# Moving three quarters of the z projection between the convolved blocks, and one exponential with one fp32 value matmul per score tile in the banded attention

## The chip, the core and the metric

The kernel runs on one core of one Trainium2 chip. The metric is device time in microseconds (us) of one execution; smaller is better. The engines are TensorE (PE, with its weight loads shown apart as PEld), VectorE (DVE), ScalarE (ACT), GpSimd (POOL) and the queue that issues nearly all transfers (SP). Each engine takes its own instructions in the order in which the program has them.

## The reference, cut to what matters

Two layers of a hybrid trunk are computed for 1024 latent tokens and 128 context tokens (1152 together, nine tiles of 128). The change lies in the first layer, whose combined input projection yields queries, keys and values, a gate, z, the convolved channels xbc and dt:

```python
q, k, v, g, z, xbc, dt = split_cols(h @ w_in, (A_WIDTH, A_KV_WIDTH, A_KV_WIDTH, A_WIDTH, SSD_INNER, CONV_CH, 2 * SSD_HEADS))
xbc = silu(centred_conv(xbc, conv_w, conv_b))          # 1280 channels, 5 taps
# (A) attention in a band of 3 blocks of 128 keys, all 128 context keys and a sink logit, in one softmax
p = softmax([s_local, s_context, s_sink]);  attn = p @ [v_window, v_context]
# (B) two chunked state scans (forwards, backwards) over the convolved channels give y
a_out = attn * silu(g)
s_out = rms_norm(y * silu(z), gnorm_w)                 # z has 1024 columns
out   = concat([a_out, s_out]) @ w_out
```

The second layer (latent attention over all keys), the residuals and the final norm follow. All data are fp32.

## The kernel before

**Precision.** A product is made "whole" by splitting both sides into a high and a low part in the type fp32r (`split`, lines 249 to 253: ACT writes the high part, DVE the rest) and by three fp32r matmuls (`mm3`, lines 256 to 258). Some products are single matmuls in plain fp32 instead.

**Memory.** SBUF is divided by hand into four arenas, R, S, G and F; `Space.tile` takes a stretch of one, with `bufs` copies in turn. An instruction that rewrites a copy waits until the readers of the old one are done. `mem.set` opens an arena anew, after everything in the old one has ended.

**Order.** The program is written as generators that are woven together, and a scheduler then places the instructions of each engine, so rows of different generators stand mixed in one queue. Once placed, an engine's order is fixed.

**The stages around the change**, with the lines of the kernel before:

- Keys and values of all tiles, and the cached ones, are made first (`put_kv`); values are split into `VH` (with a column of ones, so that the value product also gives the softmax's denominator) and `VL`, in arena G.
- *Queries and z.* `weave(queries, 18, zproj, 36)` puts two z tiles beside each of 18 query tiles. A query tile (`query_tile`) is a projection of 24 matmuls of 256 columns, the rotation on DVE and POOL, a split, four transposes (L643), a copy by ACT (L644), eight score products `pp` (L660, L661), four maxima on DVE (L663), three small DVE steps (L667 to L669), and two small transposes (L672, L673) that write the negated maximum and the sink's exponential. A z tile (`zproj`) is 24 matmuls of 256 columns, a tanh (L686), one DVE step (L687) and a store; it is needed only in the scan.
- *Convolved blocks with attention.* `convs` runs over ten blocks of 128 channels. A block is three chunks of 24 matmuls of 384 columns (`fm_proj`), copied by ACT into the single buffer `ub` (L856 to L859), then a first tap on ACT (L878), four taps on DVE (L880), a tanh, transposes (L892), and chunk products of the states (`chunk_states`, L808, L812), whose results go to `H_d` (L840). Between blocks come pieces of `modulation` (L355, L356). Beside it runs `attention0`: per tile and key head two to four key blocks, each with a score tile of 128 by 512 (L740, L742, L743), two exponentials of the same score tile (L747 into fp32, L748 into fp32r), their difference `pl` (L749, on DVE or POOL in turn, one buffer), and three value matmuls into `acco` (L751 to L753). Three steps of attention go with one block. Its denominators go through memory (`den_d`, then `rd_d`).
- *Gates and first scans.* `gates0` makes 12 gate products. Each needs a chunk of matmuls (`fm_proj`, then the tanh of L713), the attention's output `ot` and a broadcast of `rd_d` into `rb` (L950; two buffers of `ot`, one of `rb`), a product on POOL (L951) and one on DVE (L953). `scan_out` for the context tile and the first latent tile is woven in, and `out_weights` loads the output weights.
- *Scans and output projection.* For each tile `scan_out` and `project_out`; the first transposes of `norm_T` (L1049) end the first tile of it.

The names in the rows are the arenas or the tiles: `acc` is a projection's PSUM tile, `sc` a score tile, `acco` the attention's sum, `pp` a score tile for the maxima, `st` the chunk states, `pt` a transpose.

Of the kernel before, what the change touches and what calls it, by code (L numbers as in the profile page):

```python
# [12 lines left out]
F32 = mybir.dt.float32  # L13
# [7 lines left out]
D = 1024  # L21
# [7 lines left out]
R_COLS, S_COLS, G_COLS, F_COLS = 27136, 4352, 11168, 9136  # L29
# [191 lines left out]
def hybrid_trunk(ctx: ExitStack, tc: tile.TileContext, I, O, dbg=None, stage=99):  # L221
# [243 lines left out]
    VH = kvp.tile([128, NB, 2, 65], F32R, name="VH", at="G")  # L465
    VL = kvp.tile([128, NB, 2, 64], F32R, name="VL", at="G")
    pool.memset(VH[:, :, :, 64:65].bitcast(F32), 1.0)

# [73 lines left out]
    with Space(mem) as p:  # L542
# [22 lines left out]
        def put_kv(p, blk, kr, vsrc):  # L565
# [12 lines left out]
            split(VH[:, blk, :, 0:64], VL[:, blk], vsrc.rearrange("p (h d) -> p h d", h=2))  # L578
# [102 lines left out]
        def zproj(zp, w):  # L681
            for q in range(4):
                for t in range(NT):
                    acc = tok_proj(t, w, 256)
                    th = zp.tile([128, 256], F32, tag="zth", name="zth", bufs=3)
                    act.activation(th, acc, AF.Tanh)  # L686
                    dve.scalar_tensor_tensor(th, th, 1.0, acc, ALU.add, ALU.mult)  # L687
                    dma.dma_start(z_d[t * 128:(t + 1) * 128, q * 256:(q + 1) * 256], th)
                    if t == 6 and q < 3:
                        wn = zw(q + 1)  # L690
                    yield
                w = wn

        with Space(mem) as qp:
            wp.widen("wh", "wl")
            weave(queries(qp, wq), 18, zproj(qp, wz), 36)

    if stage <= 2:
        dbg("KV", KH.bitcast(F32), KL.bitcast(F32), VH.bitcast(F32), VL.bitcast(F32), qm_d, es_d, dts)
        return  # L700
# [16 lines left out]
    def attention0(p):  # L717
# [4 lines left out]
        for t in range(NT):  # L722
            tok = slice(t * 128, (t + 1) * 128)
            for kv in range(2):
# [13 lines left out]
                for n, (kb, msk) in enumerate(blocks):  # L738
# [8 lines left out]
                    act.activation(pf, sc, AF.Exp, scale=SCALE_A)  # L747
                    act.activation(ph, sc, AF.Exp, scale=SCALE_A)  # L748
                    (pool if n % 2 else dve).tensor_tensor(pl, pf, ph.bitcast(F32), ALU.subtract)  # L749
                    vh = VH[:, kb, kv]  # L750
                    pe.matmul(acc[0:65], vh, ph, start=(n == 0), stop=False)  # L751
# [95 lines left out]
    def convs(p):  # L847
# [18 lines left out]
        for n, sb in enumerate(order):  # L866
            for b in range(2):
                w = ws.pop(0)
                ws.append(cw(2 * n + b + 2))
                for c in range(NCH):  # L870
                    evac(c, fm_proj(w, 0, hT, c))
                    for _ in range(4 + c):
                        next(beside, None)
# [816 lines left out]
```

## Time and profile before

| | |
|---|---|
| time of three runs | 1856.84, 1853.19, 1844.75 us; median 1853.19 us |
| profiled execution | 1854.25 us, its span 1852.5 us |
| PE busy | 1734.0 us (94%) in 9031 matmuls |
| DVE, ACT, POOL busy | 1043.6, 819.9, 744.5 us |
| mean granted TensorE clock | 0.956 |

The profile is one execution. A group row names the line, the engine, the operation, what it writes and reads, the count, then the busy time, the mean duration of one and the idle time ahead of it with what ended that. A row of the timeline gives the start in us from the span's start and the duration in us. Ends of matmuls are modelled and overlap with the next one, so what a matmul costs is read from the distance between starts. A plain fp32 matmul shows as two records, an fp32r matmul as one.

### The profile page before, as it was taken

To read this page: it belongs to the slowest core of one execution; us is meant where nothing else is said; L and a number is where in the kernel's file an instruction comes from. 1 tells how busy PE (TensorE), PEld (TensorE's weight loads), DVE (VectorE), ACT (ScalarE), POOL (GpSimd) and SP (SyncE) were. 2 spreads that over 40 slices of the span, in tenths; PEclk is the share of its full clock that TensorE was granted. 3 is DMA by queue.
4 is the path that set the end of the run, shared out by engine and by line. 5 is a ranking of instruction groups with operands and counts; after the bars stand their busy time and mean duration, and the time that the engine had idled before them with its cause. 6 is when DMAs were issued, how large, how long until landed. Compare 5 with 4: busy or idle time off the path is not lost.

```text
span 1852.5 us, 27066 instructions
## 1 busy us (share of the span) xinstructions
PE 1734.0 (94%) x9031; PEld 1314.2 (71%) x9031; DVE 1043.6 (56%) x1989; ACT 819.9 (44%) x1873; POOL 744.5 (40%) x741
## 2 busy tenths in 40 slices
PE   6899999999998888989899999999999999999898
PEld 3799999877775776767688898655565665554486
DVE  5665545655545467677665434655655556565243
ACT  5532323665655354444444422444544544545321
POOL 3510000133333345575633010456565575476432
PEclk9999999999998888998999998899999999999999
DMA  7423323444435697464463532020120121113352
GB/s 259 124 84 92 118 67 107 130 115 122 122 92 146 201 288 241 163 207 146 157 186 85 166 113 79 17 55 23 45 77 24 40 62 46 43 34 113 95 165 91
DMA packets 210655, 210.26 MB, mean 114 GB/s; under 512 B 36162, under 2 KB 175504, under 8 KB 210516
## 3 DMA queue, kind: packets, MB, share of 16 engines
q1 hardware_dynamic: 210372, 208.40, 37.6%
q8 instruction: 72, 1.18, 0.3%
q14 instruction: 67, 0.55, 0.1%
q0 software_dynamic: 144, 0.13, 0.0%
HBM read 151.94 MB, written 51.72 MB: 110 GB/s over the span
## 4 chain that ended last, share of the span: by engine, by line
PE 67%; DMA 11%; DVE 6%; ACT 3%; POOL 3%; issue 2%; SPq 2%; POOLq 0%; DVEq 0%; ACTq 0%
PE acc L256 12%; PE acc L258 12%; PE acc L257 12%; PE acco L1465 6%; PE pp L1427 3%; PE sc L1448 3%; PE sc L1450 3%; PE sc L1449 3%; DMA arenaG<-cum_d 2%; DMA arenaF<-rd_d 2%; DVE arenaR L250 2%; DMA arenaG<-rd_d 2%; PE st L808 1%; DMA rd_d<-arenaF 1%; PE yacc L1011 1%
## 5 line engine op out<-in xcount | busy, mean ns | idle before, releaser
L256 PE MATMUL acc<-arenaR 128*128 128x384 f32 (+4 forms) x1248 | 427.4, 343 | 19.4 <-ACT arenaR L249 9.1
L1478 POOL TENSOR_TENSOR arenaG<-arenaG 128x512 f32<-128x512 f32 x256 | 331.0, 1307 | 245.1 <-ACT arenaG L1455 178.8
L257 PE MATMUL acc<-arenaR 128*128 128x384 f32 (+3 forms) x1176 | 398.7, 339 | 0.1
L258 PE MATMUL acc<-arenaR 128*128 128x384 f32 (+4 forms) x1152 | 387.6, 338 | 0.2
L256 PEld LDWEIGHTS acc<-arenaR 128*128 128x128 f32 x1248 | 241.4, 194 | 60.8 <-ACT arenaR L249 11.6
L1455 ACT ACTIVATE arenaG<-sc 128x512 f32<-128x512 f32 (+1 forms) x304 | 175.5, 581 | 223.5 <-PE sc L1450 209.9
L209 DVE TENSOR_REDUCE arenaF<-pp 128x1 f32<-128x384 f32 (+1 forms) x400 | 198.5, 540 | 116.9 <-PE pp L1427 115.9
L257 PEld LDWEIGHTS acc<-arenaR 128*128 128x128 f32 x1176 | 226.8, 193 | 14.6 <-issue 2.7
L258 PEld LDWEIGHTS acc<-arenaR 128*128 128x128 f32 x1152 | 222.8, 193 | 16.6 <-DVE arenaR L250 2.2
L1465 PE MATMUL acco<-arenaG 128*64 128x512 f32 (+1 forms) x608 | 162.5, 614 | 1.1 <-ACT arenaG L1455 1.1
L250 DVE TENSOR_TENSOR arenaR<-arenaF,arenaR 128x512 fp32r<-128x512 f32 (+2 forms) x135 | 113.0, 851 | 60.5 <-ACT arenaR L249 55.9
L1005 ACT ACTIVATE arenaG<-arenaG,arenaF 128x128 f32<-128x128 f32 x288 | 88.7, 392 | 117.8 <-POOL arenaG L1003 117.5
L249 ACT CAST arenaR<-arenaF 128x512 fp32r<-128x512 f32 (+3 forms) x151 | 91.8, 626 | 92.3 <-DMA arenaF<-in_ab_w_in_dram 23.9
L749 POOL TENSOR_TENSOR arenaG<-arenaF,arenaG 128x512 fp32r<-128x512 f32 x28 | 48.4, 1728 | 149.8 <-PE acco L753 78.3
L1427 PE MATMUL pp<-arenaR 96*128 96x384 f32 (+1 forms) x300 | 96.1, 391 | 8.1 <-DVE arenaF L209 7.9
L1427 PEld LDWEIGHTS pp<-arenaR 96*128 96x128 f32 x300 | 57.9, 202 | 63.2 <-issue 27.3
L1448 PE MATMUL sc<-arenaR 96*128 96x512 f32 (+1 forms) x228 | 96.7, 424 | 3.6 <-ACT arenaG L1455 3.6
L258 PE MATMUL acc<-arenaR,arenaS 128*128 128x512 f32 (+1 forms) x240 | 92.2, 389 | 0.0
L1450 PE MATMUL sc<-arenaR 97*128 97x512 f32 (+1 forms) x228 | 89.9, 398 | 1.0 <-DMA arenaR<-arenaF 1.0
L1449 PE MATMUL sc<-arenaR 96*128 96x512 f32 (+1 forms) x228 | 89.4, 392 | 0.0
L1003 POOL TENSOR_SCALAR_AFFINE_SELECT arenaG<-arenaG 128x512 f32<-128x512 f32 x72 | 60.9, 869 | 65.7 <-DMA arenaG<-cum_d 53.4
L1448 PEld LDWEIGHTS sc<-arenaR 96*128 96x128 f32 x228 | 43.6, 191 | 59.5 <-ACT arenaG L1455 42.1
(328 smaller groups left out, 3362.7 us busy)
## 6 DMA issues: line engine op xcount, KB each, us to landing
arenaF<-in_ada_w_dram SPq DMA_DIRECT2D x96, 256.0 KB
arenaG<-cum_d SPq DMA_DIRECT2D x36, 512.0 KB
arenaF<-in_ab_w_in_dram SPq DMA_DIRECT2D x51, 256.0 KB
z_d<-arenaF SPq DMA_DIRECT2D x36, 128.0 KB
xs_d<-arenaF SPq DMA_DIRECT2D x8, 576.0 KB
arenaF<-xs_d SPq DMA_DIRECT2D x9, 512.0 KB
arenaF<-z_d SPq DMA_DIRECT2D x9, 512.0 KB
x_d<-arenaG SPq DMA_DIRECT2D x9, 512.0 KB
```

The lines of the kernel that those rows point to most:

```text
L209: f()
L250: lo_eng.tensor_tensor(lo, src, hi.bitcast(F32), ALU.subtract)
L256: pe.matmul(out, ah, bh, start=first, stop=False)
L257: pe.matmul(out, ah, bl, start=False, stop=False)
L258: pe.matmul(out, al, bh, start=False, stop=last)
L1427: pe.matmul(pp[:, 0:w], AQ[s][0:96, t * 128:(t + 1) * 128], AK[s][0:96, k0:k0 + w], start=True, stop=True)
L1448: pe.matmul(sc[:, 0:n], AK[s][0:96, ks], BQ[s][:, qs], start=True, stop=False)
L1449: pe.matmul(sc[:, 0:n], BK[s][:, ks], AQ[s][0:96, qs], start=False, stop=False)
L1450: pe.matmul(sc[:, 0:n], AK[s][:, ks], AQ[s][:, qs], start=False, stop=True)
L1455: act.activation(pf, sc[:, 0:n], AF.Exp, scale=SCALE_M)
L1465: (pinned if a == 0 else lambda f: f())(lambda: pe.matmul(acc[0][a * 64:(a + 1) * 64], V[:, a], pfs[a], start=(i == 0), stop=last))
L1478: pool.tensor_tensor(totals[a], first[a] if i == 1 else totals[a], pfs[a], ALU.add)
```

## The change

Five things are done together.

1. z: only the first quarter of its columns (256) stays beside the queries, so `weave` has 9 z tiles instead of 36. The other 768 columns are made in six blocks of 128 inside `convs`, one after each of the convolved blocks number 2 to 7 of ten: three chunks of 24 matmuls of 384 columns (`fm_proj`), tanh and DVE step on 128 by 384, three transposes per chunk, a copy by ACT into `zt`, and a store. The weights come as slabs of 128 columns in one list with those of the convolved blocks.
2. Attention: one exponential into fp32 (three buffers), no difference, and one plain fp32 value matmul per key block instead of three fp32r ones.
3. Values: one fp32 tile `VV` in arena F (copied by ACT) instead of `VH` and `VL` in G.
4. Two steps of attention instead of three go with one step of `convs`.
5. Arena G has 8576 instead of 11168 columns and F the 2592 more; three tiles and one reservation of the second layer may lie in G or F.

```diff
-R_COLS, S_COLS, G_COLS, F_COLS = 27136, 4352, 11168, 9136
+R_COLS, S_COLS, G_COLS, F_COLS = 27136, 4352, 8576, 11728
...
-    VH = kvp.tile([128, NB, 2, 65], F32R, name="VH", at="G")
-    VL = kvp.tile([128, NB, 2, 64], F32R, name="VL", at="G")
+    vvp = Space(mem, right=True)
+    VV = vvp.tile([128, NB, 2, 65], F32, name="VV")
...
-            split(VH[:, blk, :, 0:64], VL[:, blk], vsrc.rearrange("p (h d) -> p h d", h=2))
+            act.copy(VV[:, blk, :, 0:64], vsrc.rearrange("p (h d) -> p h d", h=2))
...
         def zproj(zp, w):
-            for q in range(4):
-                for t in range(NT):
-                    acc = tok_proj(t, w, 256)
...
+            for t in range(NT):
+                acc = tok_proj(t, w, 256)
...
-            weave(queries(qp, wq), 18, zproj(qp, wz), 36)
+            weave(queries(qp, wq), 18, zproj(qp, wz), 9)
...
-                    pf = p.tile([128, 512], F32, tag="pf", name="pf", bufs=2)
-                    ph = p.tile([128, 512], F32R, tag="ph", name="ph", bufs=2)
-                    pl = p.tile([128, 512], F32R, tag="pl", name="pl", bufs=1)
+                    pf = p.tile([128, 512], F32, tag="pf", name="pf", bufs=3)
                     act.activation(pf, sc, AF.Exp, scale=SCALE_A)
-                    act.activation(ph, sc, AF.Exp, scale=SCALE_A)
-                    (pool if n % 2 else dve).tensor_tensor(pl, pf, ph.bitcast(F32), ALU.subtract)
-                    vh = VH[:, kb, kv]
-                    pe.matmul(acc[0:65], vh, ph, start=(n == 0), stop=False)
-                    pe.matmul(acc[0:64], VL[:, kb, kv], ph, start=False, stop=False)
-                    pe.matmul(acc[0:65], vh, pl, start=False, stop=(n == len(blocks) - 1))
+                    pe.matmul(acc[0:65], VV[:, kb, kv], pf, start=(n == 0), stop=(n == len(blocks) - 1))
...
-        cw = lambda n: slab(w0, 2304 + blocks[n] * 128, 128, bufs=3) if n < 10 else gate_weights(n - 10)
-        ws = [cw(0), cw(1)]
+        todo = [slab_of for n in range(10) for slab_of in [(2304 + blocks[n] * 128, None)] + ([(1280 + (n + 1) * 128, 0.5)] if 0 < n < 7 else [])]
...
+        def z_block(b, w):
+
+            def turn(c, th):
+                pt = psum("tr", "pt")
+                for i in range(3):
+                    pe.transpose(pt[:, i * 128:(i + 1) * 128], th[:, i * 128:(i + 1) * 128], ident)
+                zt = p.tile([128, 3, 128], F32, tag="zt", name="zt", bufs=1)
+                act.copy(zt, pt[:, 0:CH].rearrange("p (t c) -> p t c", t=3))
+                dma.dma_start(z_d.rearrange("(t p) c -> p t c", p=128)[:, c * 3:c * 3 + 3, b * 128:(b + 1) * 128], zt)
+            for c in range(NCH):
+                acc = fm_proj(w, 0, hT, c)
+                if turns:
+                    turns.pop()()
+                th = p.tile([128, CH], F32, tag="zth", name="zth", bufs=2)
+                act.activation(th, acc, AF.Tanh)
+                dve.scalar_tensor_tensor(th, th, 1.0, acc, ALU.add, ALU.mult)
+                turns.append(partial(turn, c, th))
...
                 some_modulation(p, 2 if b and n < 2 else 1)
                 yield
+                if 0 < 2 * n + b < 7:
+                    w = ws.pop(0)
+                    next_weights()
+                    z_block(2 * n + b + 1, w)
+                    yield
...
-            done = [next(at, StopIteration) is StopIteration for _ in range(3)]
+            done = [next(at, StopIteration) is StopIteration for _ in range(2)]
...
-            tiles.append(p7.tile([128, NKT, 2, 64], F32, tag="vv", name="vv", bufs=3, at="G"))
+            tiles.append(p7.tile([128, NKT, 2, 64], F32, tag="vv", name="vv", bufs=3, at="GF"))
```

The scheduler places the instructions, so three places of its order are shown, before and after. In the rows a line number is that of the kernel the row is of; in the changed kernel the score matmuls are L736, L738 and L739, the value matmul L742, z's transposes L870, the taps L900, the attention output's load L976 and the broadcast of `rd_d` L978.

**The query stage's end.** Before, PE between two query tiles, with z's matmuls (here the 256-column rows) on both sides of the transposes of one query tile:

```order
L256 MATMUL acc<-arenaS,arenaR 128x256
L672 MATMUL pt<-ident,arenaS 4x128
L643 MATMUL pt<-ident,arenaG 128x128 x4
L673 MATMUL pt<-ident,arenaF 4x128
L257 MATMUL acc<-arenaS,arenaR 128x256
L258 MATMUL acc<-arenaS,arenaR 128x256
```

After, PE in the last five query tiles: the last score products of one tile, the transposes, and the score products of the next:

```order
L660 MATMUL pp<-arenaG,arenaR 128x384
L661 MATMUL pp<-arenaG,arenaR 128x128
L672 MATMUL pt<-ident,arenaS 4x128
L643 MATMUL pt<-ident,arenaG 128x128 x4
L673 MATMUL pt<-ident,arenaF 4x128
L660 MATMUL pp<-arenaG 128x256
L661 MATMUL pp<-arenaG 128x128
```

After, DVE at the same place: the last maxima of the query stage's last latent tile, its small steps, and the taps of the first convolved block (L900), with the context tile's maximum (L653) among them:

```order
L663 ISA arenaF<-pp,arenaF 128x384
L663 ISA arenaF 128x1
L667 SCALAR_TENSOR_TENSOR arenaF<-arenaF 128x4
L668 TENSOR_SCALAR arenaS<-arenaF 128x4
L669 SCALAR_TENSOR_TENSOR arenaF<-arenaS,arenaF 128x4
L900 SCALAR_TENSOR_TENSOR arenaF<-arenaF,vecs 128x1154 x2
L653 TENSOR_REDUCE arenaF<-pp 128x4
L900 SCALAR_TENSOR_TENSOR arenaF<-arenaF,vecs 128x1154
```

The projections have gone from between the last query tiles; five chunks of the first two convolved blocks stand ahead of them instead, and the sixth behind them.

**The attention among the convolved blocks.** Before, PE with the value matmuls of two key blocks, and scores:

```order
L753 MATMUL acco<-arenaG 65x512
L751 MATMUL acco<-arenaG 65x512
L752 MATMUL acco<-arenaG 64x512
L740 MATMUL sc<-arenaR,arenaG 128x512
L743 MATMUL sc<-arenaG 128x512
```

After, PE with the value matmuls of two key blocks, transposes of a z block between them, scores of two key blocks, and a chunk of a projection:

```order
L742 MATMUL acco<-arenaF 65x512
L870 MATMUL pt<-ident,arenaF 128x128 x3
L742 MATMUL acco<-arenaF 65x512
L736 MATMUL sc<-arenaR,arenaG 128x512
L738 MATMUL sc<-arenaG 128x512
L739 MATMUL sc<-arenaG 128x512
```

Three value rows have become one, and z's transposes stand among them.

**The first loads of the gates.** Before, SP from results of the last convolved blocks (`H_d`, `xs_d`) to the first load for a gate (L948); the first broadcast of `rd_d` (L950) follows 12 rows later:

```order
L840 DMA H_d<-arenaS 64x8x128 x2
L895 DMA xs_d<-arenaF 128x9x128
L759 DMA o_d<-arenaS 64x2x128 x2
L764 DMA arenaF<-den_d 64x16
L301 DMA arenaG<-in_ab_w_in_dram 128x4x128
L948 DMA arenaG<-o_d 128x384
```

After, SP from the last denominators to the first broadcasts (L978), with weight loads of the input projection (`in_ab_w_in`) and of the modulation (`in_ada_w`) still among them:

```order
L753 DMA arenaF<-den_d 64x16
L301 DMA arenaF<-in_ab_w_in_dram 128x4x128 x2
L976 DMA arenaG<-o_d 128x384 x2
L757 DMA rd_d<-arenaF 64x16
L301 DMA arenaF<-in_ada_w_dram 128x2x256
L978 DMA arenaG<-rd_d 64x3x128
```

The broadcasts of three gate products stand ahead of the last two stores of z blocks (L873) now, and of the last stores of `H_d`. PE has the attention's last value matmul (L742) in the first chunk of the last three convolved blocks, where the last one (L753) stood behind all of them before.

More of the change, by code (lines that the diff above doesn't have):

```diff
@@ L681, in zproj @@
         def zproj(zp, w):
-            for q in range(4):
-                for t in range(NT):
-                    acc = tok_proj(t, w, 256)
[L685 to L692, printed above, removed]
+            for t in range(NT):
+                acc = tok_proj(t, w, 256)
+                th = zp.tile([128, 256], F32, tag="zth", name="zth", bufs=3)
+                act.activation(th, acc, AF.Tanh)
+                dve.scalar_tensor_tensor(th, th, 1.0, acc, ALU.add, ALU.mult)
+                dma.dma_start(z_d[t * 128:(t + 1) * 128, 0:256], th)
+                yield
         with Space(mem) as qp:
             wp.widen("wh", "wl")
-            weave(queries(qp, wq), 18, zproj(qp, wz), 36)
+            weave(queries(qp, wq), 18, zproj(qp, wz), 9)
     if stage <= 2:
-        dbg("KV", KH.bitcast(F32), KL.bitcast(F32), VH.bitcast(F32), VL.bitcast(F32), qm_d, es_d, dts)
+        dbg("KV", KH.bitcast(F32), KL.bitcast(F32), VV, qm_d, es_d, dts)
         return
@@ L863, in convs, with next_weights @@
         blocks = [sb * 2 + b for sb in order for b in range(2)]
-        cw = lambda n: slab(w0, 2304 + blocks[n] * 128, 128, bufs=3) if n < 10 else gate_weights(n - 10)
-        ws = [cw(0), cw(1)]
+        todo = [slab_of for n in range(10) for slab_of in [(2304 + blocks[n] * 128, None)] + ([(1280 + (n + 1) * 128, 0.5)] if 0 < n < 7 else [])]
+        def next_weights():
+            if todo:
+                c0, scale = todo.pop(0)
+                ws.append(slab(w0, c0, 128, scale=scale, bufs=3))
+            elif len(gws) < 2:
+                gate_weights(len(gws))
+        ws = []
+        next_weights(), next_weights()
+        turns = []
+        def z_block(b, w):
[11 more added lines that the diff above has]
+                th = p.tile([128, CH], F32, tag="zth", name="zth", bufs=2)
+                act.activation(th, acc, AF.Tanh)
+                dve.scalar_tensor_tensor(th, th, 1.0, acc, ALU.add, ALU.mult)
+                turns.append(partial(turn, c, th))
+                for _ in range(2 + c):
+                    next(beside, None)
         for n, sb in enumerate(order):
@@ L868, in convs @@
                 w = ws.pop(0)
-                ws.append(cw(2 * n + b + 2))
+                next_weights()
                 for c in range(NCH):
                     evac(c, fm_proj(w, 0, hT, c))
+                    if turns:
+                        turns.pop()()
                     for _ in range(4 + c):
@@ L898, in convs @@
                 yield
+                if 0 < 2 * n + b < 7:
+                    w = ws.pop(0)
+                    next_weights()
+                    z_block(2 * n + b + 1, w)
+                    yield
         yield from beside
@@ L916, in hybrid_trunk @@
     kvp.close()
+    vvp.close()
     if stage <= 3:
@@ L940, in hybrid_trunk @@
     wp.widen("wh", "wl", place=1)
+    for k in ("wh", "wl"):
+        wp.rings[k][1] = 0
     def gates0(p):
@@ L1453, in pair_main @@
                     steps.tick()
-                    pf = p7.tile([128, 512], F32, tag="pf", name="pf", bufs=6, at="G")[:, 0:n]
+                    pf = p7.tile([128, 512], F32, tag="pf", name="pf", bufs=6, at="GF")[:, 0:n]
                     act.activation(pf, sc[:, 0:n], AF.Exp, scale=SCALE_M)
@@ L1476, in rest @@
                             if i == 1:
-                                totals[a] = p7.tile([128, 512], F32, tag="pt", name="pt1", bufs=4, at="G")[:, 0:n]
+                                totals[a] = p7.tile([128, 512], F32, tag="pt", name="pt1", bufs=4, at="GF")[:, 0:n]
                             pool.tensor_tensor(totals[a], first[a] if i == 1 else totals[a], pfs[a], ALU.add)
@@ L1613, in hybrid_trunk @@
                     p9.reserve("at8", 2 * D, 1, None, F32R)
[L1614 removed]
+                    p9.reserve("or8", D, 2, "FG")
                 for _ in pair_main(pair, op, CHUNKS[c:c + 1]):
```

3 lines of the change are left out of this document (1 added, 2 removed).

## Prediction

> **What bounds the kernel now.** I read the page's shares first, then the five stretches from the queries to the first scans, then single rows.
>
> ```profile
> PE 1734.0 (94%) x9031; PEld 1314.2 (71%) x9031; DVE 1043.6 (56%) x1989; ACT 819.9 (44%) x1873; POOL 744.5 (40%) x741
> 106.00:314.00 208.00, 207.74 (x1653) 205.54 (x1654) 111.29 (x339) 61.42 (x175) 13.93 (x20) 1.00 0.31 93
> 314.00:555.00 241.00, 231.66 (x1268) 184.78 (x1268) 134.35 (x200) 144.92 (x285) 72.85 (x71) 0.99 0.40 115
> 555.00:590.00 35.00, 30.10 (x156) 21.69 (x155) 21.46 (x44) 21.93 (x43) 14.48 (x14) 0.90 0.46 124
> 590.00:710.00 120.00, 99.96 (x476) 83.87 (x475) 69.79 (x114) 53.04 (x126) 48.01 (x52) 0.83 0.80 237
> 710.00:746.00 36.00, 31.23 (x138) 23.46 (x137) 23.97 (x33) 16.28 (x45) 19.57 (x20) 0.86 0.74 239
> ```
>
> Columns of the stretches: bounds, length, busy time and count of PE, PEld, DVE, ACT and POOL, granted PE clock, DMA share, GB/s. PE bounds the kernel, but not evenly. Beside the queries (106 to 314) it has no gap; in the convolved blocks (314 to 555) it lacks 9.3 us; from 590 on it idles a sixth of the time at a clock of .83, while the transfers are busiest. So a matmul added before 555 costs its whole time, and what the kernel can win lies behind 555. What paces that end:
>
> ```profile
> L859 ACT COPY arenaF<-acc x10: 250/272/299, 301.9 to 554.6; 128x128 f32<-128x128 f32 x10
> L951 POOL TENSOR_TENSOR arenaG<-arenaG x12: 993/1056/1447, 610.4 to 707.9; 128x384 f32<-128x384 f32 x12
>   DMA arenaG<-rd_d: 34.6, 9
> L953 DVE TENSOR_TENSOR arenaG<-arenaG x12: 545/558/957, 611.5 to 708.9; 128x384 f32<-128x384 f32 x12
> L950 SPq DMA_DIRECT2D arenaG<-rd_d x24: 574/593/1561, 604.0 to 702.0; - x24
> L840 SPq DMA_DIRECT2D H_d<-arenaS x16: 580/596/637, 407.2 to 661.6; - x16
> L1049 PE MATMUL pt<-ident,arenaG x72: 270/273/421, 742.9 to 972.7; 128*128 128x128 f32 x72
> ```
>
> The numbers after the count are shortest, mean and longest in ns, then first and last start. The last convolved chunk leaves PE at 554.6. Of the gate products, 9 of 12 wait 34.6 us on POOL for the broadcast of rd_d, which has one buffer; they come (708.9 − 611.5)/11 = 8.85 us apart. Two chains end at L1049, 742.9: the gates, 34.0 us after the last L953, and the states, whose last store starts 107.0 us after the last chunk and leaves 81.3 us more.
>
> **What PE gets to do.** Costs come from starts, as ends overlap:
>
> ```profile
> 149.92 0.28 PE L256 MATMUL acc<-arenaS,arenaR 128*128 128x256 f32 x1
> 150.04 0.28 PE L257 MATMUL acc<-arenaS,arenaR 128*128 128x256 f32 x1
> 396.49 0.34 PE L258 MATMUL acc<-arenaR 128*128 128x384 f32 x1
> ...
> 397.90 0.33 PE L257 MATMUL acc<-arenaR 128*128 128x384 f32 x1
> 399.77 0.39 PE L753 MATMUL acco<-arenaG 128*65 128x512 f32 x1
> 400.00 0.40 PE L751 MATMUL acco<-arenaG 128*65 128x512 f32 x1
> 400.23 0.40 PE L752 MATMUL acco<-arenaG 128*64 128x512 f32 x1
> 400.47 0.34 PE L256 MATMUL acc<-arenaR 128*128 128x384 f32 x1
> 406.91 1.04 PE L892 MATMUL pt<-ident,arenaS 128*128 128x128 f32 x8
> 407.70 0.47 PE L753 MATMUL acco<-arenaG 128*65 128x512 f32 x1
> 739.47 2.08 PE L992 MATMUL off<-arenaG,arenaF 64*128 64x512 f32 x4
> 741.48 0.79 PE L256 MATMUL acc<-arenaR,arenaS 128*128 128x512 f32 x1
> 1501.80 1.08 PE L1465 MATMUL acco<-arenaG 128*64 128x512 f32 x4
> 1502.81 0.44 PE L1427 MATMUL pp<-arenaR 96*128 96x384 f32 x1
> ```
>
> *z.* A 256-column matmul takes .12 us. Of 384 columns, eight lie from 396.49 to 397.90, .176 each. Gone are 27 z tiles × 24 × .12 = 77.8 us; new are 18 chunks × 24 × .176 = 76.0 and 54 transposes, by L892's eight from 406.91 to 407.70 at .10, 5.3. Net +3.5.
>
> *Values.* Three fp32r matmuls (399.77 to 400.47) take .70 us. One plain fp32 matmul of 512 columns is two records: L992's four records, two matmuls, took 2.01 us together, 1.0 each. The narrow L1465 gives a lower end: its four records, two matmuls, took 1.01 together, but the two fill 64 columns each of the array side by side; each alone costs between .51 (its share) and 1.01 (if a neighbour is free). I take L992, the nearer in shape (full 512 columns, no neighbour): .31 more on each of 62 blocks, +19.2. The bounds are −12 (.51) and +21 (2.08/2, L992's busy time).
>
> The Trainium skill, page "FP8 and Floating Point Precision", section "TensorE Precision Notes", says that true FP32 takes four passes through the array. By that rule, four of the .23 us passes make .92, an estimate, +14 us instead of +19; this trace's 1.0 is a little above it. Either way three passes become about four.
>
> **The query stage loses its filler.** z stays beside only the first query tiles; five of the last have no projection between them.
>
> ```profile
> 150.16 0.34 PE L660 MATMUL pp<-arenaG 128*128 128x384 f32 x1
> 151.20 0.22 PE L661 MATMUL pp<-arenaG 128*128 128x128 f32 x1
> 153.57 0.17 DVE L668 TENSOR_SCALAR arenaS<-arenaF 128x4 fp32r<-128x4 f32 x1
> 156.22 0.27 PE L672 MATMUL pt<-ident,arenaS 128*4 128x128 f32 x1
> 156.33 0.60 PE L643 MATMUL pt<-ident,arenaG 128*128 128x128 f32 x4
> 156.97 0.59 ACT L644 CAST arenaR<-pt 128x512 fp32r<-128x512 f32 x1 [2.79 <-PE pt L643]
> L663 DVE CUSTOM_DVE_ANT_0 arenaF<-pp,arenaF 128x512 f32<-128x512 f32 (+1 forms) x64 | 38.8, 654 | 11.5 <-PE pp L661 11.0
> L880 DVE SCALAR_TENSOR_TENSOR arenaF<-arenaF,vecs 128x1154 f32<-128x1154 f32 x36 | 54.1, 1503 | 6.2 <-ACT arenaF L878 4.8 <-DMA arenaG<-qs_d 1.2
> ```
>
> One tile's loop is: first score product to the small step L668, 153.57 + .17 − 150.16 = 3.58; transposes, 156.97 − 156.22 = .75; the copy, .59: 4.9, with semaphores 5.0. PE has 1.8 of work in it (products 1.26, transposes some .5), and nothing else stands there in its order: 3.2 us idle, three times, 9.6 (I take the first two of the five as covered by what the queue still holds). The last tile is worse, since on DVE three taps of the first convolved block stand behind its last maxima, and the sixth chunk's buffer comes free only after them: four maxima at .65 and small steps, 3.6 in all, then four taps at 1.50, 6.0, and 1.2 for the buffer's copy and first tap, less 2.5 us of PE's own work there, is 8.3. Together +18. It is 0 if the five chunks ahead run late enough to cover them, and 24 at most (five tiles at 3.2 + the last).
>
> **The convolved stage gets its waits back.**
>
> ```profile
> L753 PE MATMUL acco<-arenaG x62: 387/397/690, 326.2 to 586.9; 128*65 128x512 f32 x62
>   POOL arenaG L749: 16.9, 10
>   DVE arenaG L749: 3.1, 9
> L747 ACT ACTIVATE arenaF<-sc 128x512 f32<-128x512 f32 x62 | 37.2, 600 | 31.8 <-POOL arenaG L749 17.8 <-DVE arenaG L749 9.7 <-PE sc L743 4.0
> 555.00:590.00 35.00, 3.96 (x9) 1.36 (x9) 0.90 0.46 124
> ```
>
> The third value matmul waits 20.0 us for the difference pl, mostly for POOL. That goes, and with it 62 of the exponentials of .6 and all differences. What is late next is the one exponential after the scores, behind z's 18 tanhs, copies and DVE steps on the same engines; ACT was busy 145 of 241 us here and ends lower. I take back 16 of the 20, since an exponential that ACT does late still stops PE; bounds 8 and 20.
>
> One thing more moves: 9 of 62 L753 ran behind the last chunk (the last row is the stretch 555 to 590 for L753 alone). With three score matmuls of the same width, 9 × (.70 + .69) = 12.5 us of PE work now come before it.
>
> So the last chunk leaves PE at 554.6 + 3.5 + 19.2 + 12.5 + 18 − 16 = **591.8**, 37.2 us later.
>
> **The end stage gains more than that.** Because the attention ends ahead of the last three blocks, three gate products have their loads issued before the last z stores and need only their chunk. *Gates:* of twelve, nine are left at 8.85 from the last chunk on, with 6 us to the first (the loads alone, without the 17 us of den_d and rd_d round trip): 6 + 79.7 = 85.7, at 677.5; then 34.0 as before, and 10 for work that PE did while it waited for broadcasts and now has left over (half of the 20 us that it idled from 590 to 710): 721.5. *States:* their last store came 107.0 after the chunk, with nine attention steps and all gates' weight loads between; the steps are gone, PE's idle there (20 of 120 us at .83) is partly closed, and I put it at 60, then 74 of the 81.3 as cum_d's loads start earlier: 591.8 + 134 = 725.8. That 60 is the softest number here, between 35 (only the states' own work, the stretch to 590) and 107 (nothing gained). The later of the two decides: 725.8 against 742.9, **−17.1**.
>
> *At nothing:* the values' split, now one ACT copy per tile, lies beside projections that PE works through without a gap (106 to 314); if that cover failed it would be a copy of .6 on nine tiles, 5. The smaller arena G costs the scans and the second layer nothing as long as no tile waits for an older reader longer than now; no row shows that, and I bound it by ±10. What follows L1049 has the same instructions and moves as a whole.
>
> 1854.25 − 17.1 = 1837.1 on the profiled execution; that one lies 1.1 above the median of three, so **1836**.
>
> **Rivals.** About 1% (18.5 us) is what a measurement of this kernel tells from no change; the forecast sits on that line.
>
> *More gain (chance .18).* The scheduler's five chunks really cover the query tiles, the 18 us go, and all behind comes 18 sooner: 1818. For: PE has no gap at all beside queries now. Against: the order's rows, where score products of one tile follow the transposes of the last with nothing between.
>
> *No gain (.16).* The transfers bind the end. From 590 to 746 the queues moved 120 us × 237 + 36 × 239 GB/s = 37 MB, at the highest DMA share of the five stretches; the change takes none of it away. At 237 GB/s from 591.8 it takes 156 us, to 747.8, 4.9 later than now: 1858. For: the broadcasts waited for are transfers. Against: in 314 to 590 the share is under .5, so what is issued earlier has room.
>
> *Slower (.16).* The first broadcast of rd_d still comes after the last chunk. Then the twelve are served as before: 17 us (604.0 − 586.9) of round trip, 12 × 8.85 = 106 and 44, from 596 (591.8 and the attention's last steps): 763, +20: 1873. It decides from the moment the first gate product on POOL starts later than the last chunk. Against it stand SP's rows; for it, that SP's rows only say what is issued in order, and a weight load ahead that waits for its buffer holds all behind.
>
> **Numbers.** Forecast .50, own range 1806 to 1850: below, values at .51 (−31 against my 1.01) bring 1805, say 1806; above, the tail at 24 and waits at 8 bring 1836 + 6 + 8. Half of it lies over the 1% bound of 1834.7. The range goes from 1806 to 1868, the no-gain rival and the arenas' 10: it holds the first two rivals and leaves out the slower one and a few ends, under .2. Faster .25 + .18 = .43; same .25 + .16 = .41; slower .16.
>
> **What would show it.** Value matmuls 1.0 apart in two records; PE gaps of 3 us between L661 and L672 in the last queries, 8 ahead of a chunk; waits of the value matmul under 4 us in all; the last L859's successor at 585 to 600; three gate products on POOL before it; L1049 near 726. Wrong if the first gate product lies behind the last chunk, if the chunk comes past 605, or if the arenas' new split (G is 2592 columns narrower) makes scans or the second layer wait for buffers, of which this trace shows nothing.

## The result, and the profile after

The changed kernel took **1912.33 us** (median of 4 runs, 1909.35 to 1915.84): 1.031 times the kernel before, 95% interval 1.027 to 1.035. I had forecast 1836, a gain of 1%; it lost 3%, outside my range. Times here and below are medians that leave out two slow executions, one each of the kernels with two buffers for `rd_d` and with a single broadcast. The profiled execution took 1909.35 us, its span 1907.2.

The stages, from the view of time stretches (bounds, length, busy time and count of PE, PEld, DVE, ACT, POOL, granted PE clock, DMA share, GB/s). First after:

```profile
PE 1758.0 (92%) x8807; PEld 1323.3 (69%) x8807; DVE 1009.4 (53%) x1936; ACT 798.3 (42%) x1820; POOL 692.6 (36%) x713
106.00:280.00 174.00, 148.86 (x1004) 139.55 (x1005) 94.04 (x300) 44.72 (x136) 13.83 (x20) 0.88 0.25 74
280.00:622.70 342.70, 336.47 (x1781) 273.94 (x1779) 135.31 (x223) 162.49 (x320) 44.65 (x55) 0.98 0.42 120
622.70:783.40 160.70, 132.66 (x662) 109.28 (x661) 102.47 (x159) 70.01 (x165) 67.84 (x71) 0.86 0.75 215
783.40:1025.10 241.70, 216.35 (x996) 168.51 (x995) 155.35 (x198) 97.95 (x271) 120.29 (x130) 0.90 0.52 164
```

Then before, the stretches that were not shown yet, cut at the same events: last convolved chunk, first and last transposes of `norm_T`.

```profile
314.00:554.60 240.60, 231.26 (x1266) 184.55 (x1266) 133.95 (x198) 144.69 (x285) 72.83 (x70) 0.99 0.41 116
554.60:742.90 188.30, 158.59 (x752) 126.58 (x750) 113.50 (x188) 89.24 (x207) 81.07 (x84) 0.85 0.73 218
742.90:972.70 229.80, 211.32 (x997) 165.63 (x996) 158.47 (x198) 100.14 (x279) 128.07 (x131) 0.93 0.55 171
```

Idle PE is length less busy time. What the clock costs I take as half of the time that PE is busy in the spans of half clock that the trace lists. The rest is work at full clock:

| stage (us) | before | after | difference | of it PE work | idle PE | half clock |
|---|---|---|---|---|---|---|
| 106 to the last chunk | 448.6 | 516.7 | +68.1 | +28.2 | +21.8 | +18.2 |
| to `norm_T`'s first transposes | 188.3 | 160.7 | −27.6 | −17.2 | −1.7 | −8.7 |
| scans, to its last | 229.8 | 241.7 | +11.9 | +2.1 | +6.9 | +2.9 |
| the rest | 879.8 | 882.1 | +2.3 | | | |

The milestones, by line: the last chunk's copy (L848), the gate products (L979), the states' stores (L829), `norm_T` (L1077).

```profile
L848 ACT COPY arenaF<-acc x10: 268/272/285, 236.3 to 622.7; 128x128 f32<-128x128 f32 x10
L979 POOL TENSOR_TENSOR arenaG<-arenaG x12: 992/1014/1443, 582.9 to 746.0; 128x384 f32<-128x384 f32 x12
  DMA arenaG<-rd_d: 15.3, 5
L829 SPq DMA_DIRECT2D H_d<-arenaS x16: 574/601/1477, 388.1 to 687.0; - x16
L1077 PE MATMUL pt<-ident,arenaG x72: 270/273/475, 783.4 to 1025.1; 128*128 128x128 f32 x72
```

**Where the query stage lost it.** The timeline of PE in the last query tiles (start, duration; in brackets the idle time before it and what ended it):

```profile
251.06 0.27 PE L672 MATMUL pt<-ident,arenaS 128*4 128x128 f32 x1 [2.33 <-DVE arenaS L668]
...
254.72 0.31 PE L661 MATMUL pp<-arenaG 128*128 128x128 f32 x1
256.55 0.37 PE L672 MATMUL pt<-ident,arenaS 128*4 128x128 f32 x1 [1.52 <-DVE arenaS L668]
256.71 1.06 PE L643 MATMUL pt<-ident,arenaG 128*128 128x128 f32 x4
257.57 0.42 PE L673 MATMUL pt<-ident,arenaF 128*4 128x128 f32 x1
258.45 0.69 PE L660 MATMUL pp<-arenaG,arenaR 128*128 128x384 f32 x1 [0.46 <-ACT arenaR L644]
...
274.32 0.37 PE L672 MATMUL pt<-ident,arenaS 128*4 128x128 f32 x1 [2.07 <-DVE arenaS L668]
...
275.30 0.52 PE L257 MATMUL acc<-arenaR 128*128 128x384 f32 x1
275.62 0.52 PE L258 MATMUL acc<-arenaR 128*128 128x384 f32 x1
...
279.49 0.34 PE L257 MATMUL acc<-arenaR 128*128 128x384 f32 x1
279.67 0.34 PE L258 MATMUL acc<-arenaR 128*128 128x384 f32 x1
140.00:220.00 80.00, 66.80 (x483) 63.26 (x481) 42.85 (x148) 18.05 (x58) 7.45 (x11) 0.91 0.24 71
251.40:278.70 27.30, 18.56 (x66) 14.56 (x65) 15.86 (x43) 6.98 (x21) 0.00 (x0) 0.50 0.26 76
```

The waits are those that I forecast, on DVE's small step L668 and ACT's copy L644. What I had left out is their second price: for 27.3 us (the last row) the clock is .50, and a matmul of 384 columns starts every .32 us (275.30 to 275.62) where it later takes .18. The wait of 3.2 us that I worked out per tile is 2.0 of idle PE here (1.52 + .46): of the 5.8 us from one L672 to the next (256.55 to 262.36) PE's own work takes 3.8, twice the 1.8 that I had. Nor is it the last tiles only: from 140 to 220 (the last row but one), while some z tiles still stood beside the queries, PE lacks 13.2 of 80 us at a clock of .91, with four spans of half clock of 3.4 us each.

### The profile page after: what moved, and what is told of

Same layout as the page of the kernel before. It is cut to its first block, busy times and chain, and to the rows that moved or that the text cites. A ratio compares the mean times of both kernels' runs of the same rounds, so it can differ in the third digit from the quotient of the medians.

```text
span 1907.2 us, 26407 instructions
## 1 busy us (share of the span) xinstructions
PE 1758.0 (92%) x8807; PEld 1323.3 (69%) x8807; DVE 1009.4 (53%) x1936; ACT 798.3 (42%) x1820; POOL 692.6 (36%) x713
## 3 DMA queue, kind: packets, MB, share of 16 engines
HBM read 151.94 MB, written 51.72 MB: 107 GB/s over the span
## 4 chain that ended last, share of the span: by engine, by line
PE 33%; DMA 8%; DVE 3%; ACT 3%; SPq 2%; issue 2%; POOL 0%; DVEq 0%; POOLq 0%; ACTq 0%
PE acco L1493 5%; PE acc L256 5%; PE acc L257 5%; PE acc L258 5%; PE pp L1455 3%; PE sc L1476 3%; PE sc L1478 3%; PE sc L1477 2%; DMA arenaF<-rd_d 2%; DMA arenaF<-in_mla_w_in_dram 1%; DMA rd_d<-arenaF 1%; ACT arenaR L249 1%; DMA arenaF<-in_mla_w_out_dram 1%; PE den L1522 1%; DVE arenaF L1300 1%
## 5 line engine op out<-in xcount | busy, mean ns | idle before, releaser
L256 PE MATMUL acc<-arenaR 128*128 128x384 f32 (+4 forms) x1248 | 440.8, 354 | 36.0 <-ACT arenaR L249 11.0
L257 PE MATMUL acc<-arenaR 128*128 128x384 f32 (+3 forms) x1176 | 409.6, 348 | 0.1
L258 PE MATMUL acc<-arenaR 128*128 128x384 f32 (+4 forms) x1152 | 399.4, 347 | 0.1
L1506 POOL TENSOR_TENSOR arenaG<-arenaG 128x512 f32<-128x512 f32 x192 | 248.6, 1306 | 233.0 <-ACT arenaG L1483 166.1
L256 PEld LDWEIGHTS acc<-arenaR 128*128 128x128 f32 x1248 | 243.6, 195 | 79.7 <-issue 22.9
L250 DVE TENSOR_TENSOR arenaR<-arenaF,arenaR 128x512 fp32r<-128x512 f32 (+2 forms) x140 | 121.3, 882 | 126.1 <-ACT arenaR L249 125.2
L785 POOL TENSOR_TENSOR arenaS<-arenaF 128x256 f32<-128x256 f32 x72 | 57.8, 826 | 326.3 <-ACT arenaF L913 165.4
L249 ACT CAST arenaR<-arenaF 128x512 fp32r<-128x512 f32 (+3 forms) x156 | 98.0, 646 | 149.5 <-DMA arenaF<-in_ada_w_dram 29.0
L1455 PEld LDWEIGHTS pp<-arenaR 96*128 96x128 f32 x300 | 57.8, 202 | 63.2 <-DVE arenaF L209 25.6
L250 DVE TENSOR_TENSOR arenaR<-acc,arenaR 64x384 fp32r<-64x384 f32 (+2 forms) x84 | 48.1, 578 | 58.2 <-ACT arenaR L249 57.3
L1033 ACT ACTIVATE arenaF<-arenaF 128x128 f32<-128x128 f32 x144 | 44.7, 389 | 77.7 <-POOL arenaF L1031 77.7
```

The costliest lines, as they stand in the source:

```text
L250: lo_eng.tensor_tensor(lo, src, hi.bitcast(F32), ALU.subtract)
L256: pe.matmul(out, ah, bh, start=first, stop=False)
L257: pe.matmul(out, ah, bl, start=False, stop=False)
L258: pe.matmul(out, al, bh, start=False, stop=last)
L1455: pe.matmul(pp[:, 0:w], AQ[s][0:96, t * 128:(t + 1) * 128], AK[s][0:96, k0:k0 + w], start=True, stop=True)
L1506: pool.tensor_tensor(totals[a], first[a] if i == 1 else totals[a], pfs[a], ALU.add)
```

## Experiments

Ratios are to the kernel before, with 95% intervals. "Stage" numbers are from each run's profile, cut at the same three events.

**z back beside the queries.**

```diff
-            weave(queries(qp, wq), 18, zproj(qp, wz), 9)
+            weave(queries(qp, wq), 18, zproj(qp, wz), 36)   # zproj of before
-                if 0 < 2 * n + b < 7:
+                if False:
-            done = [... for _ in range(2)]
+            done = [... for _ in range(3)]
```

> The changed kernel with z wholly beside the queries again (36 tiles) and three attention steps a block; the attention and the arenas stay changed. Theory 'filler' (the query stage of the changed kernel lost 25.1 us to idle PE and 15.4 us to the halved clock, 40.5 together): the last convolved chunk leaves PE 44 us or more earlier than its 622.7, at 565 to 580, and the kernel takes 1860 to 1878 us. Rival 'attention' (the plain fp32 value matmuls and the narrower arena make the loss): the kernel stays at 1895 us or above.

1857.21 us, **1.0036** (1.0014 to 1.0058). The stretch before the last chunk fell from 516.7 to 464.4 us; 'filler' holds, and the total is 3 us below its range.

```profile
106.00:316.00 210.00, 209.57 (x1666) 207.28 (x1666) 111.93 (x340) 62.53 (x181) 13.87 (x20) 1.00 0.31 93
570.40:733.10 162.70, 139.46 (x697) 113.70 (x696) 100.92 (x163) 74.30 (x173) 68.84 (x73) 0.87 0.74 218
```

PE has no gap in the first row, as before the change. The second says something that I had not asked: the end stage is as short (162.7) as in the changed kernel (160.7). So it does not need z between the blocks, and the next run shows that it does not need the new attention either. The attention's part of the change costs .36% with z beside the queries, and z's move the rest: 1.0309 / 1.0036 = 1.027.

**The z move alone.** The kernel before with the changed kernel's `zproj`, `z_block` and list of slabs, and two attention steps to a block; `zth` and `o` with one buffer.

> The kernel before with the z move alone: attention with two exponentials, a difference and three value matmuls, arenas of before, two attention steps to one of the blocks (to make room, z's tanh tile and the attention's sum copy have one buffer). Theory 'filler': the query stage loses about 40 us as in the changed kernel, and the total is 1880 to 1900 us. Rival 'attention': within 10 us of the kernel before, 1845 to 1865. A side question, the 12 us lost in the last scan tile: if they come from the narrower arena G, they are absent here and present in the kernel with z back.

1888.95 us, **1.0223** (1.0180 to 1.0266). As 'filler' had it:

```profile
106.00:281.00 175.00, 149.36 (x1019) 140.07 (x1018) 95.81 (x303) 45.30 (x138) 13.79 (x20) 0.89 0.25 73
618.10:766.00 147.90, 130.09 (x677) 106.19 (x675) 102.58 (x158) 69.97 (x165) 69.25 (x71) 0.93 0.78 233
766.00:1006.60 240.60, 216.32 (x994) 166.24 (x995) 156.11 (x199) 98.21 (x271) 120.75 (x130) 0.90 0.53 164
```

25.6 us idle and 14.1 lost to the clock in the first row. The side question is answered too: the scans (last row) took 240.6 us with the wide arena G of before, and 229.7 with the narrow one in the run with more work below, so the narrower arena is not what lengthened them. What the 236.6 with z back come from is not shown.

The end stage (second row) is 147.9 us with the old attention, shorter than in the changed kernel. What the short ones share is when the attention ends. Its last value matmul starts ahead of the last chunk's copy in all three: at 523.8 against 570.4 with z back, 558.4 against 618.1 here, 562.3 against 622.7 in the changed kernel. In the kernel before, 9 of 62 run behind it. That is the step that I forecast, but no run changes it alone.

**Half of z beside the queries.**

```diff
-            weave(queries(qp, wq), 18, zproj(qp, wz), 9)
+            weave(queries(qp, wq), 18, zproj(qp, wz), 18)   # two quarters
-                if 0 < 2 * n + b < 7:
+                if 0 < 2 * n + b < 5:
```

> The changed kernel with half of z (18 tiles) beside the 18 query tiles and half in four blocks among the convolved ones. Theory 'filler': each query tile finds one z tile, the query stage's 40.5 us of idle and halved clock fall to some 20, and the kernel takes 1885 to 1895 us. Rival 'tail' (only the last tiles without any z lose, 18 us as I had it): the nine z tiles more fill the last tiles too, the loss goes nearly whole, and the time is near that of the kernel with z wholly back.

1875.24 us, **1.0145** (1.0095 to 1.0195), 10 us less than 'filler' had and 18 more than with z wholly back, where 'tail' had it. The query stage decides for 'filler', which had some 20 there. Idle and clock cost it 16.2 + 7.5 = 23.7 us, between 40.5 with 9 tiles and .4 with 36:

```profile
106.00:289.00 183.00, 166.78 (x1228) 159.70 (x1228) 99.43 (x314) 50.36 (x152) 13.98 (x20) 0.93 0.27 82
```

**More work that costs little.** 27 z tiles of matmuls whose results nothing reads, beside the queries of the changed kernel:

```diff
+                for _ in range(3):
+                    tok_proj(t, w, 256)
+                    yield
-            weave(queries(qp, wq), 18, zproj(qp, wz), 9)
+            weave(queries(qp, wq), 18, zproj(qp, wz), 36)
```

> The changed kernel with 27 more z tiles of matmuls beside the queries whose results nothing reads (they repeat the first quarter): PE gets 27 x 24 x .12 = 77.8 us of work more. Theory 'gaps' (in the query stage 25.1 us of PE are idle and 15.4 lost to the halved clock, and any matmul fills them): the query stage grows by 37, from 174 to about 211 us with no idle PE and a full clock, the total from 1912 to about 1949. Rival 'chain' (the query tiles' own chain over DVE and ACT takes as long whatever PE does between): the stage grows by 60 or more, the total to 1975 or above.

1926.74 us, 1.0405 (1.0369 to 1.0440): 77.8 us of added work cost 14.4 by the medians, and 26.6 between the spans of the two profiled executions (1933.8 against 1907.2).

```profile
106.00:308.00 202.00, 201.57 (x1627) 199.61 (x1626) 92.36 (x300) 44.88 (x138) 13.55 (x20) 1.00 0.21 64
818.00:1047.70 229.70, 210.33 (x998) 165.21 (x997) 151.58 (x198) 98.48 (x272) 120.38 (x130) 0.93 0.55 172
```

The query stage has no idle PE and a full clock; up to the last chunk the kernel grew by 551.3 − 516.7 = 34.6, as 'gaps' had it (37). Its total, 1949, was too high: the scans gave 12.0 back (second row: 229.7, as before the change), and what follows them took 4.0 more. In this run the last load of `cum_d` stands ahead of a store on SP (1004.42 and 1006.84); the next runs are about that order.

**The scans: a load behind a store.** The queue SP in the changed kernel, at the last loads of `cum_d` (L1028):

```profile
965.74 0.32 SPq L1028 DMA_DIRECT2D arenaF<-cum_d  x1
968.37 0.33 SPq L1110 DMA_DIRECT2D arenaG<-in_x_sample_dram  x1
973.28 0.37 SPq L1082 DMA_DIRECT2D h_d<-arenaF  x1
979.17 0.32 SPq L1028 DMA_DIRECT2D arenaG<-cum_d  x1
```

and from the waits of 955 to 1005:

```profile
POOL arenaG L1031 <- DMA arenaG<-cum_d: 12.1, 1, 12.1
```

The last load stands behind `norm_T`'s store of `h_d`. In the kernel before, the two stand the other way round (cum_d at 931.15, h_d at 933.57). Stores moved to ACT's queue:

```diff
-            dma.dma_start(h1_d[q * 4:q * 4 + 4, :, tok]..., full)
+            act.dma_start(h1_d[q * 4:q * 4 + 4, :, tok]..., full)
```

> The changed kernel with the stores of h_d by norm_T issued on ACT's queue instead of SP's. In the changed kernel the last load of cum_d stands on SP behind such a store, which waits for norm_T, and is issued 13.4 us after the one ahead of it (5.9 in the kernel before). Theory 'behind the store': the stage from norm_T's first to its last transpose falls from 241.7 us to 230 or so, and the total by 8 to 12 us. Rival (the load waits for its buffer, not for the store): within 4 us of the changed kernel.

1887.68 us, 1.0175 (1.0132 to 1.0219), 24 us below the changed kernel, twice what I expected.

```profile
955.19 0.32 SPq L1028 DMA_DIRECT2D arenaF<-cum_d  x1
958.76 0.33 SPq L1110 DMA_DIRECT2D arenaG<-in_x_sample_dram  x1
960.58 0.32 SPq L1028 DMA_DIRECT2D arenaG<-cum_d  x1
780.70:1003.30 222.60, 208.47 (x998) 162.29 (x997) 152.60 (x198) 97.32 (x271) 121.96 (x130) 0.95 0.55 177
```

The last two loads are 5.4 us apart instead of 13.4, and the scans take 222.6 instead of 241.7. Of these 19.1 us 11.2 are idle PE and 8.1 half clock, with the same PE work. Of all runs with the stores on SP, only the changed kernel and the z move alone have this order, and theirs are the two longest scans (241.7, 240.6; the others 225.4 to 238.9). With the output weights' bytes left out they took 238.9 in the good order, so the order isn't the only thing that sets them, and how much of the 24 us it makes by itself is not shown. In the kernel before, the move brought less:

> The kernel before with the h_d stores on ACT's queue, nothing else. In the changed kernel this shortened the scans from 241.7 to 222.5 us and the total by 24. Theory 'store': the kernel before has the same wait, smaller: its scans fall from 229.8 to about 220, the total to 1838 to 1845, faster than before by 0.5 to 0.8%. Rival (only the changed kernel's order had the last cum_d behind a store): within 4 us of before.

1846.80 us, .9974 (.9955 to .9994); its scans went from 229.8 to 227.4 only. The rival is nearer: most of the 24 us belonged to the changed kernel.

**The end stage: what paces the gate products?** My step said the broadcast of `rd_d`, with its one buffer. Two buffers:

```diff
-R_COLS, S_COLS, G_COLS, F_COLS = 27136, 4352, 8576, 11728
+R_COLS, S_COLS, G_COLS, F_COLS = 26752, 4352, 8960, 11728
+    p4.widen("rb", at="G")
```

> The changed kernel with two buffers for the broadcast of rd_d instead of one (384 columns moved from arena R to G). Theory 'broadcast' (my step: gate products come one by one at the pace of one buffer): the gate products' pace falls from 12.5 us to 9 or less, the stage from the last chunk to the first transposes of norm_T from 160.7 us to 140 or less. Rival 'mixed queue' (the products wait because every engine's order has the states, the modulation and the first scans between them): pace and stage within 8 us of the changed kernel.

1893.21 us, 1.0204 (1.0163 to 1.0245). The stage fell by 7.5 to 153.2, the products' pace from 12.5 to 10.7 us: 'mixed queue' by both numbers. The total fell by more, 19 us, since the scans took 231.5 instead of 241.7, with the load ahead of the store again. The same holds for the two runs with a single broadcast, so the stage and not the total is compared.

The output weights' bytes left out:

```diff
-            raw = raw_block([128, 1, 512], wo[k * 128:(k + 1) * 128, q * 512:(q + 1) * 512].unsqueeze(1))
+            dma.dma_start(raw[:, 0:16], wo[k * 128:(k + 1) * 128, q * 512:q * 512 + 16])
...
```

The split then repeats the 16 columns, so the output projection still runs, with other weights; the program reads 6.1 MB less (145.85 instead of 151.94).

> The changed kernel, but the 24 loads of output projection weights bring 16 of 512 columns each and the split repeats them (5.9 MB fewer; the output projection of the first layer is not computed). Theory 'transfers' (the stage from the last chunk to the first transposes of norm_T moves at 215 to 218 GB/s before and after, so its bytes set its length): the stage falls from 160.7 us by 20 to 27. Rival 'chain' (broadcasts of rd_d into one buffer and the products behind them set it): by less than 6 us.

1896.57 us, 1.0256 (1.0221 to 1.0292). The stage: 152.0, 8.7 less; neither theory's number.

The broadcasts left out but for the first, and then both:

```diff
+            if (c, b) == (2, 0):
+                rb = p.tile(...)
                 for par in range(2):
                     dma.dma_start(rb[par * 64:(par + 1) * 64], ...)
```

> The changed kernel with the broadcast of rd_d loaded for the first gate product only and used by all twelve (the denominators of the other eleven are left out). Theory 'broadcast' (my step, in full: the products' pace is that of the broadcasts): pace 7 us or less, the stage from the last chunk to norm_T's first transposes 130 us or less (160.7). Rival 'mixed queue': the pace stays above 10 us, the stage above 148, as with two buffers (153.2).

1893.86 us, 1.0224 (1.0192 to 1.0255).

> Both left out: the eleven broadcasts of rd_d and the output weights' bytes (16 of 512 columns loaded). If two loads in the same queue are the bound, the gains add or more: 160.7 less 8.8 less that of the one broadcast, 135 or below. If each only uncovers the next chain (states, modulation, scans of the first tiles), the stage stays at 145 or above.

1886.47 us, 1.0170 (1.0113 to 1.0227). The end stages of the four, in the order told:

```profile
620.10:773.30 153.20, 134.23 (x687) 109.84 (x685) 101.95 (x159) 71.02 (x167) 69.64 (x71) 0.90 0.78 227
622.60:774.60 152.00, 130.55 (x661) 107.68 (x659) 96.33 (x154) 66.80 (x157) 67.00 (x70) 0.89 0.62 179
621.50:772.80 151.30, 131.77 (x657) 107.34 (x655) 101.79 (x155) 67.71 (x157) 67.28 (x69) 0.89 0.70 211
620.90:768.70 147.80, 129.36 (x665) 106.28 (x664) 101.97 (x158) 67.07 (x157) 66.90 (x69) 0.90 0.59 175
```

With a single broadcast, the products still come 10.8 us apart, as 'mixed queue' had it; without either load, and with the transfers at .59 of their time, the stage is 147.8. 'Broadcast' and 'transfers' as the bound are out: each uncovers the next chain some 9 us below. What holds the rest (115 to 122 us of PE work at full clock in 148 to 161 us) stays open; that the products wait because states, modulation and scans stand between them in the queues fits, but was not shown by a run of its own.

**Toward a better version.** Two rb buffers with z back:

> The kernel with z wholly beside the queries and the changed attention, with two buffers for the broadcast of rd_d. Theory 'broadcast': 15 us or more below that kernel with one buffer (1857 us median, 1.0036 of before), 1835 to 1843, faster than both kernels. Rival 'mixed queue': within 8 us of it, 1850 to 1865.

1851.08 us, .9988 (.9969 to 1.0007), 6 us below z back with one buffer by the medians, 9 by the ratios: 'mixed queue' again. Its end stage is 162.8 us, as with one buffer (162.7); the gain lies in the scans (225.4 against 236.6). With ACT's queue for `h_d` besides:

> z wholly beside the queries, the changed attention, two buffers for the broadcast of rd_d, h_d stores on ACT's queue. With two buffers alone it stood at 0.9988 of before. Theory 'store': 6 to 12 us less, 1839 to 1845. Rival: its scans were already 225.4 us, so no more than 3 us are left there.

1849.05 us, .9993 (.9974 to 1.0011): the rival; nothing was left there. The kernel before with four attention steps to a block:

```diff
-            done = [next(at, StopIteration) is StopIteration for _ in range(3)]
+            done = [next(at, StopIteration) is StopIteration for _ in range(4)]
```

> The kernel before with four instead of three attention steps to one convolved block, all else as before. It asks what an attention that ends earlier is worth by itself. Theory 'moved work' (PE work that goes from behind the last chunk to ahead of it gives back in the end stage about what it costs, over the efficiency of that stage: 12.5/0.7 = 18 against 12.5): the last chunk comes up to 13 us later, the end stage is shorter by 18, total 1843 to 1852. Rival: the attention stalls more on its difference pl ahead of the chunks, and the total is 1855 or above.

1847.36 us, .9979 (.9956 to 1.0003). The total is as expected, its reason isn't: the last chunk came not later but 17 us earlier, at 537.6, and the end stage grew to 195.9, with 12 value matmuls behind the chunk instead of 9. As the interval holds 1, a gain is not shown.

```profile
  POOL arenaG L749: 9.2, 11
537.60:733.50 195.90, 159.09 (x785) 127.53 (x784) 113.05 (x195) 96.52 (x228) 75.97 (x87) 0.88 0.71 209
```

The value matmuls' wait for POOL's differences fell to 9.2 us from 16.9 (first row, from the waits of L753, which add PE's and its weight loads'; PE's alone fell to 3.3 from 7.6). And both edits of the kernel before together:

> The kernel before with four attention steps to a block (0.9979 of before by itself) and the h_d stores on ACT's queue. If the two gains add: 1833 to 1841, 0.990 to 0.994 of before, the fastest here. Rival: the four steps' gain was chance of one order, and it comes to the same as the kernel before with the stores moved.

1839.32 us, **.9945** (.9924 to .9966): faster than both kernels, with neither part of the change in it, and about the sum of its two gains (.21 + .26 against .55%).

## Why the prediction was wrong, by its own steps

I had forecast 17.1 us less, and the span grew by 54.7 (1852.5 to 1907.2): some 72 apart. Four steps missed on the slow side: the end stage by 26.7, the query stage by 22.5, the waits taken back by 16, the part behind `norm_T` by 14.2. The price of a value matmul missed by 9.2 the other way, and 2 of PE work remain.

- **The query stage without filler: +18 forecast, 40.5 measured** (25.1 idle, 15.4 clock). This is the largest miss ahead of the last chunk. I saw the mechanism, and priced idle time at full clock, for the last tiles alone:

```profile
106.00:251.40 145.40, 129.00 (x934) 123.75 (x935) 78.18 (x257) 37.74 (x115) 13.83 (x20) 0.95 0.25 74
```

  From 251.4 to 278.7 the stage lost 8.7 idle and 9.3 to the clock, 18.0 together. That this is my number is luck: I had 17.9 of idle, 8.3 of it ahead of a chunk, where the gap was 2.07, and nothing for the clock. The other 22.5 lie ahead of 251.4 (16.4 idle in the row, 6.1 clock), among tiles that I had put at nothing. 'z back', 'half' and 'more work' show the cause from three sides. My rival 'more gain', that the tiles were covered, was the wrong way round.
- **The convolved stage's waits: −16 forecast, 0 measured** (idle from 9.3 to 6.2, clock from 3.4 to 6.2). I quoted that PE lacks 9.3 us between 314 and 555 and then took back 16 of 20. The 20.0 (16.9 + 3.1) was a misreading: that view adds the idle time of PE and of its weight loads. PE alone idled 8.3 us ahead of these matmuls, 5.9 of it before the last chunk:

```profile
L753 PE MATMUL acco<-arenaG 128*65 128x512 f32 x62 | 26.0, 419 | 8.3 <-POOL arenaG L749 7.6 <-DVE arenaG L749 0.7
```

  The wait did go: ahead of the new value matmul PE idles 2.0 us. That gave back the few us by which the stage's idle time fell, and the clock took them again. The row of the stretch was the bound.
- **Values: +19.2 forecast, +10 measured.** One value matmul takes .86 us, from 427.36 on:

```profile
427.36 1.02 PE L742 MATMUL acco<-arenaF 128*65 128x512 f32 x2
427.81 0.74 PE L256 MATMUL acc<-arenaR 128*128 128x384 f32 x1
428.39 0.34 PE L257 MATMUL acc<-arenaR 128*128 128x384 f32 x1
```

  428.39 − 427.36 is 1.03, less .17 for L256. The 1.0 I took from L992 was not what I made of it: it ran in a span of half clock (732.1 to 742.3), and its two matmuls have 64 rows each and start .007 us apart, side by side. The two errors nearly cancelled. The "FP8 and Floating Point Precision" page of the Trainium skill, with its four passes ("TensorE Precision Notes"), gave an estimate of .92, nearer than my row. The measured .86 decides.
- **z itself +3.5, moved attention +12.5:** with the values' 10 they make 26; PE work before the last chunk grew by 28.2. Right.
- **Last chunk: 591.8 forecast, 622.7 measured.** The three misses make it: 22.5 + 16 − 9.2, and 2 of work.
- **The end stage: 134 forecast, 160.7 measured** (188.3 before): 27.6 gained where I had 54.3, the largest miss of all. The states' last store came 64.3 us after the chunk (60 forecast), but 96.4 were left behind it, not 74. Two gate products came early, not three; the other ten came (746.0 − 633.1)/9 = 12.5 us apart, not 8.85. By the gates the stage is 10.4 us to the first of the ten, 112.9 to the last and 37.4 behind it, where I had 6, 79.7 and 44: the pace, with one product more, is the term that failed. The 8.85 was a pace of the old queue; I carried it over as if the broadcast made it, and with a single broadcast it is 10.8. What makes the pace stays open.
- **Behind `norm_T`: 0 forecast, +14.2 measured.** "The same instructions" was true and not enough: their order on SP had changed, and one load fell behind a store; with the stores on another queue the scans took 222.6 instead of 241.7. The arenas, which I had named as the risk, were not the cause.
- **The sign.** My rival on the slow side (first broadcast behind the last chunk) did not occur: the first gate product ran at 582.9. The loss against the kernel before lies ahead of the last chunk (+68.1), most of it in the query stage, the step that I had in the sum and priced at less than half; the end stage gave back only 27.6 of it.

## What to carry to other kernels

Projections beside a stage that waits on its own results are its filler: before they are moved, price the stage that they leave at half clock, for all its tiles, not only for those with nothing beside them. What a stage can give back is bounded by its idle time in the stretch view, not by a line's waits, which the view of a line adds up over PE and its weight loads, and a pace measured in one queue doesn't hold in another. After a change of order, the first place to look for a stray loss is a queue where a load has come to stand behind a store that waits.

## What the hardware did that I had not expected

PE's clock fell to half with gaps of about 2 us and less: in the stretch from 251.4 to 278.7 PE was busy 18.56 of 27.3 us, its longest wait was 2.07 us, and the clock stayed at .50 throughout. It came back at 278.7, when PE had run with no gap above .11 us since 274.3. The Trainium skill, "TensorE: Matmul & The Clock Gate" (section "Why this matters for your kernels"), asks for no idle gaps above some 3 us; this stage kept that rule (its longest gap is the 2.33 us ahead of 251.06) and lost the clock. In this stage the busy share told it as well: ahead of each of the four single spans of half clock from 159 to 214, and of the long one, PE was busy .32 to .45 of 3.4 us, and where the clock stayed full, .69 or more. The longest gaps part them too (1.88 us and more against 1.55), and the runs don't tell which counts. It is no threshold either: later in the same execution the clock fell after 3.4 us, from 1200.3, with PE busy .83.
